# A quarter of a token tile moves from dense expert products to row gathers in a one-core transformer block

## The chip, the core and the metric

The kernel runs on one core of a Trainium2 chip. The metric is device time in microseconds. The core has TensorE (PE, matmuls; PEld is its weight load), VectorE (DVE), ScalarE (ACT), GpSimd (POOL) and SyncE (SP), and 16 DMA engines that the queues of SP and POOL feed here. Engines run their own instructions in the order in which they were placed, and wait for each other by semaphores.

## The reference

One decoder block on 1024 tokens of width 1024, all in float32: adaLN and RMSNorm, a combined projection, a pooling mixer and forgetting attention, an output projection, and then the part that matters here, a product-key expert layer:

```
def peer_ffn(h, w_query, sub_keys, expert_u, expert_v):
    # 8 heads, two halves of 128 keys; top 16 of each half, then the top 16 of their sums
    # idx: (tokens, 8, 16) out of 16384 experts; gates: softmax over each head's 16
    u = expert_u[ec]                                     # (tokens, 8, 16, 1024)
    a = gelu(einsum('cd,chkd->chk', xc, u)) * wc
    return einsum('chk,chkd->cd', a, expert_v[ec])
x = x + gt2 * peer_ffn(h2, ...);  return rmsnorm(x, final_g)
```

Each token thus uses 128 of 16384 experts; each expert is one row of `peer_u` and one of `peer_v`, 4 KB each.

## The kernel before

Tokens are held in eight tiles of 128. The program has three passes over the tokens (`PHASES`: tokens 0 to 511, 512 to 767, 768 to 1023) and then one long stage, `dense_experts`.

A pass (`phase`) does projections (`proj`, 24 matmuls for each chunk of 128 output columns; float32 products are made of three products of high and low parts, `mm3`), attention, the output projection, and the scores for the expert layer (`w_query` chunks, `keys`, top 16 of each half). The next pass's head is woven into its end. What follows from the scores comes in two ways:

- For tiles inside `DT0` to `DT1` (1 to 5, 640 tokens) the experts are computed densely. `choose(tt)` picks the 128 experts of each token, `gates(gb, tt)` builds in 32 steps a token-by-expert matrix of gates from one-hot products (PE line 978, POOL line 966, ACT line 979) and writes it to `Gd` in DRAM, 1 MB after every four steps. In the dense stage `up(e)` multiplies the 640 tokens with 128 experts' u rows (48 matmuls, two halves of `NH` = 320 columns), applies gelu, multiplies with the gates `Gg`, and splits into `ah`, `al`; `down(gr, c)` multiplies these with v rows and adds into `accT`. There are 128 of each, in 16 groups of eight `up` and eight `down`. `finish_dense` transposes the result back, normalizes and stores.
- For the other tiles (0, 6, 7) `experts(tt)` gathers: 128 indirect DMAs of one u row for each of the 128 tokens (512 KB each, line 895), each followed by a product and sum on DVE (line 910) into `dots`, then 128 of v rows with a scaled sum on DVE (line 920), and the closing norm and store. Its `h2` and `acc` lie in PSUM. Gathered rows rotate through `GBUFS` + `GMORE` = 5 row buffers.

`choose`, `gates` and `experts` are generators in a list of background work, `bg["todo"]`. Each of their yields names a cost. `tick(us)`, called after each projection, attention piece and dense unit, adds `us` times `bg["rate"]` to a credit, and background pieces are taken from the front of the list while credit is left. `drain()` takes all that remains. `RATES` are the rates: second pass, third pass, dense stage, end of the third pass. The order of the list before: in the second pass choose and gates of tiles 1 to 3 (and choose of tile 0), in the third those of tiles 4 and 5, in the dense stage choose of 6 and 7, then experts of 0, 6, 7. The framework then places instructions on each engine by a timeline of its own, and DMAs marked `keep_in_program_order` keep their order.

Weights of the dense stage are loaded by SP (`load_w`, line 244: 512 KB into one of two `wr`), copied by ACT to `wh` (line 232) and split by POOL to `wl` (line 233). POOL also issues the gathers.

Of the kernel before, what the change touches and what calls it, by code (L numbers as in the profile page):

```python
# [26 lines left out]
DT0, DT1 = 1, 6  # L27
ND = (DT1 - DT0) * 128
# [3 lines left out]
GMORE = 2  # L32
# [8 lines left out]
RATES = (0.75, 0.6, 0.68, 0.7)  # L41
# [5 lines left out]
def block_kernel(ctx: ExitStack, tc: tile.TileContext, I, out, dbg=None):  # L47
# [344 lines left out]
    def head2(c):  # L392
        n, t0 = c.n, c.t0
        c.hTh = c.big.tile([128, 8, n], R, name="hTh", tag="A")
        c.hTl = c.big.tile([128, 8, n], R, name="hTl", tag="B")
        cols = (C_F,) + ((C_U, C_GA, C_GB, C_Q) if c.p == 0 else ())
        zs = to_T(c, c.xs, None, sc1, sh1, c.hTh, c.hTl, [("w_in", i) for i in cols])
        z = zs[0]
        c.pre = dict(zip(cols[1:], zs[1:]))

        zf, e1 = (c.tile("full", 3)[:16] for _ in range(2))
        nc.scalar.activation(zf, z[:16], AF.Identity, bias=bfc)
        nc.scalar.activation(e1, zf, AF.Abs)
        nc.scalar.activation(e1, e1, AF.Exp, scale=-1.0)
        nc.scalar.activation(e1, e1, AF.Ln, bias=1.0)
        nc.vector.scalar_tensor_tensor(e1, zf, 0.0, e1, op0=OP.min, op1=OP.subtract)
        nc.vector.tensor_tensor_scan(zf, e1, e1, flast, op0=OP.add, op1=OP.bypass)
        nc.vector.tensor_copy(flast, zf[:, n - 1:n])
        nc.vector.tensor_scalar(e1, zf, -1.0, None, op0=OP.mult)
        fhl = c.big.tile([48, n], R, name="fhl", tag="fhl", bufs=1)  # L410
        fh, fl = fhl[0:16], fhl[32:48]
        split(fh, fl, e1, nc.vector)
        mv(Fd[:, 0, t0:t0 + n], fh)
        mv(Fd[:, 1, t0:t0 + n], fl)
        if dbg and "F" in dbg:
            nc.sync.dma_start(dbg["F"][:, t0:t0 + n], zf)
# [64 lines left out]
    def phase(c, nxt):  # L481
# [259 lines left out]
        dl = [i for i in range(NQ) if DT0 <= qb0 + i < DT1]  # L741
        gl = [i for i in range(NQ) if i not in dl]
        if dl:
            T = slice(dl[0] * 128, dl[-1] * 128 + 128)
            o = (qb0 + dl[0] - DT0) * 128
            mv(h2dT[0][:, :, o:o + len(dl) * 128], h2h[:, :, T])
            mv(h2dT[1][:, :, o:o + len(dl) * 128], h2l[:, :, T])
            per = D // n
            for b, v in enumerate(tiles):
                mv(x1dT[:, b * per:(b + 1) * per, o:o + len(dl) * 128], v[:, :, T])  # L750
# [52 lines left out]
    def choose(tt, mv_, mx_):  # L803
        yield 0.0
        dense = DT0 <= tt < DT1
# [54 lines left out]
        gt = sel.tile([128, PH, 16], F, name="gate", tag="gated" if dense else f"gate{tt}", bufs=1)  # L860
# [20 lines left out]
        if dbg and "idx" in dbg:  # L881
            nc.sync.dma_start(dbg["idx"][tt * 128:(tt + 1) * 128], ix)
            nc.sync.dma_start(dbg["gate"][tt * 128:(tt + 1) * 128], gate[tt])

    X = {"i": 0, "p": None}
# [13 lines left out]

    def experts(tt):  # L900
        yield 0.0
        row = g_row("row")
        nc.sync.dma_start(row, h2d[tt])
        h2 = X["ps"].tile([128, D], F, name="h2", tag="gx", bufs=1)
        nc.scalar.activation(h2, row, AF.Copy)
        dots = gp.tile([128, 128], F, name="dots", tag="dots", bufs=1)
        for k in range(128):
            yield GSTEP
            g = gather(I["peer_u"], idx[tt][:, k:k + 1])
            nc.vector.scalar_tensor_tensor(g, g, 1.0, h2, op0=OP.mult, op1=OP.mult, accum_out=dots[:, k:k + 1])  # L910
# [14 lines left out]
        r1, r2 = g_row("r1"), g_row("r2")  # L925
        nc.sync.dma_start(r1, x1d[tt])
        nc.sync.dma_start(r2, I["final_g"].partition_broadcast(128))
        nc.vector.tensor_tensor(r0, r0, r1, op=OP.add)  # L928
        ss = cst.tile([128, 4], F, name="ss", tag="ssg", bufs=2)
        nc.scalar.activation(r1, r0, AF.Square, accum_out=ss[:, 3:4])  # L930
        nc.scalar.activation(ss[:, 3:4], ss[:, 3:4], AF.Sqrt, scale=1.0 / D, bias=epsc)  # L931
        nc.vector.reciprocal(ss[:, 3:4], ss[:, 3:4])  # L932
        nc.vector.scalar_tensor_tensor(r0, r0, ss[:, 3:4], r2, op0=OP.mult, op1=OP.mult)  # L933
        nc.sync.dma_start(out[tt * 128:(tt + 1) * 128, :], r0)

    def gates(gb, tt):
# [35 lines left out]
        def use(q, o1, o2):  # L972
# [8 lines left out]
            if r == 3:  # L981
                nc.sync.dma_start(Gd[:, :, (tt - DT0) * 8 + c, :].rearrange("g p x -> p g x"),
# [3 lines left out]
        for q in range(32):  # L986
# [8 lines left out]
    def dense_experts():  # L995
# [47 lines left out]
        def finish_dense(i, rows, fg):  # L1043
            ps = [f() for f in ((pt_tile, pt_tile), (z_tile, z_tile), (s_tile, s_tile))[i % 3]]
            ss = cst.tile([128, 4], F, name="ss", tag="ssd", bufs=2)
            yt = rows[:, i * D:i * D + D]
            hs = (slice(0, 512), slice(512, 1024))
            for hf, (pt, H) in enumerate(zip(ps, hs)):
                for c in range(4):
                    nc.tensor.transpose(pt[:, c * 128:(c + 1) * 128],  # L1050
                                        acc[:, hf * 4 + c, i * 128:(i + 1) * 128], ident)
                nc.scalar.activation(yt[:, H], pt, AF.Square, accum_out=ss[:, hf:hf + 1])
            rs = rstd(ss)
# [16 lines left out]
        for i in range(DT1 - DT0):  # L1070
            finish_dense(i, rows, fg[:, 0])
# [33 lines left out]
    late = [experts(tt) for tt in range(DT0)]  # L1105
    bg["todo"] = ch[:DT0] + [f for i in range(DT0, 4) for f in (ch[i], gates(gb, i))]
# [11 lines left out]
    bg["todo"] = ch + late + [experts(tt) for tt in range(DT1, 8)]  # L1118
# [60 lines left out]
```

## Time and profile before

| | us |
|---|---|
| median of 3 runs | 3370.76 (3367.56 to 3373.42) |
| the profiled execution | 3370.09 |
| its span, first to last instruction | 3368.4 |
| mean granted TensorE clock | 0.975 of full speed |

The span is cut below into stretches. The third pass ends near 1502 us, where the first matmul of 320 columns starts; the dense matmuls end near 3320 us. Busy time of PE is modelled, since matmuls are pipelined; the rate of a stretch is read from the number of matmuls in it, or from their starts. "Idle before, releaser" is the time in which an engine waited and what ended it.

### The profile page before, as it was taken

What the parts mean: (1) busy time and instruction counts of PE and PEld (TensorE: products, weight loads), DVE (VectorE), ACT (ScalarE), POOL (GpSimd) and SP (SyncE); (2) the same over time, 40 slices, a digit from 0 to 9 for tenths busy, and PEclk for the clock granted to TensorE, in tenths of its full rate; (3) what the DMA queues carried; (4) which work ended last, traced back from release to release, by engine and by line L of the source; (5) the groups of instructions that cost most, each with busy time, mean ns of one, the idle gap of its engine ahead of it and who ended that gap; (6) DMA issues with size and microseconds to landing.
All of it is one profiled execution on the core that took longest, in us unless ns stands there. A gap on an engine that the chain in (4) does not pass through costs nothing. (4 is left out here: it accounts for less than half of the span.)

```text
span 3368.4 us, 57444 instructions
## 1 busy us (share of the span) xinstructions
PE 3153.8 (94%) x21232; PEld 3014.7 (89%) x21232; DVE 2423.6 (72%) x5472; ACT 1240.8 (37%) x2317; POOL 1756.9 (52%) x1328
## 2 busy tenths in 40 slices
PE   6999989888889899888999999999999999999995
PEld 4788778788788889888999999999999999999994
DVE  5764456988858876669766777677676766777677
ACT  5545543345554565633222322232222222322231
POOL 1233233014323132323877777688776867777774
PEclk9999999899999999999999999999999999999997
DMA  8987777767788778893899899899998999999997
GB/s 328 324 294 259 274 274 288 252 223 228 241 307 279 248 243 268 264 339 132 317 333 327 326 326 336 316 355 329 336 328 318 325 336 338 345 320 336 327 337 253
DMA packets 378840, 1004.64 MB, mean 298 GB/s; under 512 B 34768, under 2 KB 151104, under 8 KB 376384
## 3 DMA queue, kind: packets, MB, share of 16 engines
q1 hardware_dynamic: 267968, 598.26, 51.6%
q0 software_dynamic: 110592, 402.70, 33.0%
q8 instruction: 168, 2.75, 0.3%
q14 instruction: 112, 0.92, 0.1%
HBM read 851.25 MB, written 149.58 MB: 297 GB/s over the span
## 5 line engine op out<-in xcount | busy, mean ns | idle before, releaser
L233 POOL TENSOR_TENSOR wl<-wr,wh 128x1024 fp32r<-128x1024 f32 x320 | 776.5, 2427 | 624.8 <-ACT wh L232 553.1
L232 ACT ACTIVATE wh<-wr 128x1024 fp32r<-128x1024 f32 x325 | 344.2, 1059 | 900.4 <-PE oT L280 520.7
L279 PE MATMUL oT<-ah,wh 128*128 128x320 f32 x2048 | 631.9, 309 | 7.5 <-ACT ah L232 7.5
L279 PE MATMUL z<-h2x,wh 128*128 128x320 f32 x2048 | 633.1, 309 | 2.4 <-ACT wh L232 1.3
L280 PE MATMUL oT<-al,wh 128*128 128x320 f32 x2048 | 632.8, 310 | 1.6 <-DVE al L233 1.6
L280 PE MATMUL z<-h2x,wh 128*128 128x320 f32 x2048 | 632.8, 309 | 0.0
L281 PE MATMUL z<-h2x,wl 128*128 128x320 f32 x2048 | 632.6, 309 | 0.1
L281 PE MATMUL oT<-ah,wl 128*128 128x320 f32 x2048 | 632.1, 309 | 0.1
L920 DVE SCALAR_TENSOR_TENSOR acc<-g,dots,acc 128x1024 f32<-128x1024 f32 x381 | 489.7, 1285 | 139.2 <-DMA g<-peer_v,idx 136.2
L910 DVE SCALAR_TENSOR_TENSOR g<-g,h 128x1024 f32<-128x1024 f32 x384 | 461.6, 1216 | 104.0 <-DMA g<-peer_u,idx 102.7
L895 POOL DMA_INDIRECT g<-peer_u,idx x384 | 361.9, 942 | 131.2 <-issue 57.4
L895 POOL DMA_INDIRECT g<-peer_v,idx x384 | 362.0, 943 | 127.5 <-issue 49.7
L279 PEld LDWEIGHTS oT<-ah,wh 128*128 128x128 f32 x2048 | 384.4, 188 | 8.3 <-ACT ah L232 8.3
L280 PEld LDWEIGHTS oT<-al,wh 128*128 128x128 f32 x2048 | 384.6, 188 | 3.0 <-DVE al L233 3.0
L279 PEld LDWEIGHTS z<-h2x,wh 128*128 128x128 f32 x2048 | 384.4, 188 | 3.1 <-ACT wh L232 1.7
L281 PEld LDWEIGHTS oT<-ah,wl 128*128 128x128 f32 x2048 | 384.6, 188 | 0.4 <-POOL wl L233 0.4
L281 PEld LDWEIGHTS z<-h2x,wl 128*128 128x128 f32 x2048 | 384.3, 188 | 0.4 <-POOL wl L233 0.4
L280 PEld LDWEIGHTS z<-h2x,wh 128*128 128x128 f32 x2048 | 384.4, 188 | 0.0
L966 POOL TENSOR_TENSOR o<-hi,lo 128x512 f32<-128x512 f32 x160 | 206.4, 1293 | 316.2 <-PE G L978 280.9
L279 PE MATMUL z<-hTh,wh 128*128 128x256 f32 (+1 forms) x840 | 288.9, 348 | 24.5 <-ACT hTh L232 8.3
L281 PE MATMUL z<-hTh,wl 128*128 128x256 f32 (+1 forms) x840 | 287.1, 342 | 3.8 <-DMA wl<-w_inl 3.8
L280 PE MATMUL z<-hTl,wh 128*128 128x256 f32 (+1 forms) x840 | 286.7, 341 | 1.4 <-DVE hTl L233 1.3
(286 smaller groups left out, 6042.3 us busy)
## 6 DMA issues: line engine op xcount, KB each, us to landing
wr<-ut SPq DMA_DIRECT2D x128, 512.0 KB
wr<-vt SPq DMA_DIRECT2D x128, 512.0 KB
Gd<-Gb SPq DMA_DIRECT2D x40, 1024.0 KB
Gg<-Gd SPq DMA_DIRECT2D x16, 2560.0 KB
wh<-w_inh SPq DMA_DIRECT2D x60, 512.0 KB
wl<-w_inl SPq DMA_DIRECT2D x60, 512.0 KB
wm<-w_mod SPq DMA_DIRECT2D x48, 512.0 KB
wr<-w_in SPq DMA_DIRECT2D x45, 512.0 KB
```

Of the source, the lines that this page charges most:

```text
L232: nc.scalar.activation(hi, src, AF.Copy)
L233: eng_lo.tensor_tensor(lo, src, hi.bitcast(F), op=OP.subtract)
L279: nc.tensor.matmul(ps, ah, bh, start=start, stop=False)
L280: nc.tensor.matmul(ps, ah, bl, start=False, stop=False)
L281: nc.tensor.matmul(ps, al, bh, start=False, stop=stop)
L895: d = nc.gpsimd.indirect_dma_start(out=g, out_offset=None, in_=table, in_offset=bass.IndirectOffsetOnAxis(ap=col, axis=0))
L910: nc.vector.scalar_tensor_tensor(g, g, 1.0, h2, op0=OP.mult, op1=OP.mult, accum_out=dots[:, k:k + 1])
L920: nc.vector.scalar_tensor_tensor(acc, g, dots[:, k:k + 1], acc, op0=OP.mult, op1=OP.add)
L966: nc.gpsimd.tensor_tensor(o2, hi[:, X, :, None].to_broadcast([128, 4, 8, 16]), lo[:, X, None, :].to_broadcast([128, 4, 8, 16]), op=OP.mult)
```

## The change

The dense products now take tokens 32 to 639 (608 tokens, halves of 304 columns). Gathered are tiles 5, 6 and 7 and tokens 0 to 31 of tile 0 (`HT`). For that quarter tile, 32 tokens lie four times on the 128 partitions, each quarter with 32 of the token's 128 experts, so that 32 + 32 gathers do it; three SBUF moves and sums then add the quarters. Its `experts` generator stands at the end of the third pass's list (after choose and gates of tile 4), with `h2` and `acc` in SBUF (`ha`) as long as the PSUM pool is not there. `choose(5)` moves from the third pass into the dense stage, where `drain()` leaves what is left of the quarter tile too. Tile 5 is now written as rows (`x1d`, `h2d`) in the second pass's end. Tile 0's `gates` begin at step 8 of 32. `GMORE` goes from 2 to 4. Two rates change.

```
-DT0, DT1 = 1, 6
-ND = (DT1 - DT0) * 128
+DA, DB = 32, 640
+HT, DT1 = 0, 5
+HK = 32
+ND = DB - DA
-GMORE = 2
+GMORE = 4
-RATES = (0.75, 0.6, 0.68, 0.7)
+RATES = (0.75, 0.65, 0.77, 0.7)
...
-        fhl = c.big.tile([48, n], R, name="fhl", tag="fhl", bufs=1)
+        fhl = c.tile("plh", 1, R)
...
         if p == 2:
-            bg["todo"].insert(0, gates(W["gb"], DT1 - 1))
             bg["rate"] = RATES[3]
...
-        dl = [i for i in range(NQ) if DT0 <= qb0 + i < DT1]
-        gl = [i for i in range(NQ) if i not in dl]
+        lo, hi = max(t0, DA), min(t0 + n, DB)
+        gl = [i for i in range(NQ) if not DA <= t0 + i * 128 <= DB - 128]
...
-        dense = DT0 <= tt < DT1
+        dense = tt < DT1
+        gathered = tt == HT or not dense
...
+    def x_tile(name):
+        if X["ps"]:
+            return X["ps"].tile([128, D], F, name=name, tag="gx", bufs=1)
+        return gp.tile([128, D], F, name=name, tag="ha", bufs=1)
+
     def experts(tt):
         yield 0.0
+        n, K = (HK, HK) if tt == HT else (128, 128)
         row = g_row("row")
-        nc.sync.dma_start(row, h2d[tt])
-        h2 = X["ps"].tile([128, D], F, name="h2", tag="gx", bufs=1)
+        ix, gt = idx[tt], gate[tt]
+        if tt == HT:
+            ix = sel.tile([128, HK], I32, name="ixh", tag="ixh", bufs=1)
+            gt = sel.tile([128, HK], F, name="gth", tag="gth", bufs=1)
+            for b in range(128 // HK):
+                to, c = slice(b * HK, b * HK + HK), slice(b * HK, b * HK + HK)
+                nc.sync.dma_start(ix[to], idx[tt][:HK, c])
+                nc.sync.dma_start(gt[to], gate[tt][:HK, c])
+                nc.sync.dma_start(row[to], h2d[tt][:HK])
+        else:
+            nc.sync.dma_start(row, h2d[tt])
+        h2 = x_tile("h2")
...
-        for k in range(128):
+        for k in range(K):
...
+        r1 = g_row("r1")
+        if tt == HT:
+            for b in range(1, 128 // HK):
+                nc.sync.dma_start(r1[:n], r0[b * n:b * n + n])
+                nc.vector.tensor_tensor(r0[:n], r0[:n], r1[:n], op=OP.add)
+                r1 = g_row("r1")
...
-        for q in range(32):
+        for q in range(DA // 4 if tt == HT else 0, 32):
...
-    late = [experts(tt) for tt in range(DT0)]
-    bg["todo"] = ch[:DT0] + [f for i in range(DT0, 4) for f in (ch[i], gates(gb, i))]
+    early = [experts(HT)]
+    bg["todo"] = [f for i in range(4) for f in (ch[i], gates(gb, i))]
     bg["rate"] = RATES[0]
     c, ch = phase(c, next_head(2))
     W["xq"].release()
-    bg["todo"] += [f for i in range(4, DT1) for f in (ch[i - 4], gates(gb, i))][:-1]
+    bg["todo"] += [ch[0], gates(gb, 4)] + early
+    late = ch[1:]
     bg["rate"] = RATES[1]
     c, ch = phase(c, lambda: None)
+    early = [f for f in bg["todo"] if f in early]
+    bg["todo"] = [f for f in bg["todo"] if f not in early]
     drain()
...
-    bg["todo"] = ch + late + [experts(tt) for tt in range(DT1, 8)]
+    bg["todo"] = early + late + ch + [experts(tt) for tt in range(DT1, 8)]
     bg["rate"] = RATES[2]
     dense_experts()
```

The rest of the diff follows from these: `rstd` and `finish_dense` take a last tile of 96 tokens, addresses in `Gd`, `h2dT` and `x1dT` start at token 32, and the gates and indices of gathered tiles share three buffers.

## Rows read from the trace of the kernel before

**Rows 1.** The page's first section, over the whole span: busy us (share of the span) x instructions of each engine.
```profile
span 3368.4 us, 57444 instructions
PE 3153.8 (94%) x21232; PEld 3014.7 (89%) x21232; DVE 2423.6 (72%) x5472; ACT 1240.8 (37%) x2317; POOL 1756.9 (52%) x1328
```

**Rows 2.** Stretches of the span. Columns: stretch, its length, busy us (x instructions) of PE, PEld, DVE, ACT and POOL, then the granted clock, the DMA share and GB/s.
```profile
1260.00:1400.00 140.00, 134.78 (x1108) 128.91 (x1107) 94.75 (x182) 80.35 (x161) 43.61 (x37) 1.00 0.82 263
1400.00:1502.00 102.00, 85.28 (x655) 82.23 (x654) 61.80 (x249) 43.07 (x83) 24.36 (x18) 0.93 0.93 330
1502.00:1600.00 98.00, 88.00 (x575) 85.40 (x575) 97.31 (x347) 33.43 (x55) 38.11 (x20) 0.97 0.41 151
1600.00:3300.00 1700.00, 1699.44 (x11586) 1698.93 (x11585) 1221.62 (x1868) 454.37 (x737) 1282.38 (x983) 1.00 0.91 330
...
3321.00:3369.00 48.00, 6.36 (x35) 5.08 (x33) 30.43 (x42) 10.21 (x29) 11.35 (x12) 0.56 0.74 247
```

**Rows 3.** What TensorE waited for between 1502 and 3321 us, the longest entry: us in total, times, longest us.
```profile
PE oT L279 <- ACT ah L232: 7.5, 3, 5.8
```

**Rows 4.** Starts of matmuls in time order, the first and the last of four unbroken series on TensorE: 95 starts of 320 columns, 18 of 256, 17 of 256 at another place, 16 of 512. Columns: start us, duration us, engine, line, tiles, shapes.
```profile
2000.05 0.31 PE L279 MATMUL z<-h2x,wh 128*128 128x320 f32 x1
...
2013.84 0.31 PE L280 MATMUL z<-h2x,wh 128*128 128x320 f32 x1
...
1188.27 0.28 PE L279 MATMUL z<-hTh,wh 128*128 128x256 f32 x1
...
1190.28 0.28 PE L281 MATMUL z<-hTh,wl 128*128 128x256 f32 x1
...
1181.03 0.28 PE L280 MATMUL z<-hTl,wh 128*128 128x256 f32 x1
...
1182.84 0.28 PE L281 MATMUL z<-hTh,wl 128*128 128x256 f32 x1
...
332.42 0.39 PE L279 MATMUL z<-hTh,wh 128*128 128x512 f32 x1
...
335.85 0.39 PE L279 MATMUL z<-hTh,wh 128*128 128x512 f32 x1
```

**Rows 5.** Groups of instructions by line and shape between 1602 and 3300 us: count | busy us, mean ns of one | idle before, releaser.
```profile
L233 POOL TENSOR_TENSOR wl<-wr,wh 128x1024 fp32r<-128x1024 f32 x242 | 585.2, 2418 | 195.2 <-ACT wh L232 193.3
L920 DVE SCALAR_TENSOR_TENSOR acc<-g,dots,acc 128x1024 f32<-128x1024 f32 x356 | 457.6, 1285 | 127.0 <-DMA g<-peer_v,idx 124.1
L910 DVE SCALAR_TENSOR_TENSOR g<-g,h 128x1024 f32<-128x1024 f32 x380 | 456.9, 1216 | 104.0 <-DMA g<-peer_u,idx 102.7
...
L895 POOL DMA_INDIRECT g<-peer_u,idx x377 | 354.9, 941 | 125.7 <-issue 56.3 <-DVE g L910 31.0 <-DVE al L233 6.6
...
L1021 DVE TENSOR_TENSOR z<-z,Gg 128x320 f32<-128x320 f32 x240 | 118.9, 496 | 54.7 <-ACT z L1019 52.8
L233 DVE TENSOR_TENSOR al<-z,ah 128x320 fp32r<-128x320 f32 x240 | 116.7, 487 | 22.7 <-ACT ah L232 22.7
L1037 DVE TENSOR_TENSOR accT<-accT,oT 128x320 f32<-128x320 f32 x234 | 113.2, 485 | 162.3 <-PE oT L281 162.2
...
L910 DVE DVE_READ_ACCUMULATOR g<-g,h 128x1 f32 x380 | 31.5, 83 | 0.0
```

**Rows 6.** Waits between 1600 and 3300 us: VectorE for gathered v rows, GpSimd for a row buffer that VectorE still reads.
```profile
DVE acc L920 <- DMA g<-peer_v,idx: 124.1, 109, 4.3
...
POOL g L895 <- DVE g L910: 31.6, 58, 2.7
```

**Rows 7.** Two stretches of the dense stage behind the change from one gathered tile to the next; columns as in rows 2.
```profile
2200.00:2280.00 80.00, 80.00 (x547) 80.00 (x546) 62.66 (x119) 24.09 (x43) 65.59 (x51) 1.00 0.99 369
2200.00:2300.00 100.00, 100.00 (x684) 100.00 (x683) 75.87 (x143) 27.27 (x46) 80.23 (x63) 1.00 0.96 357
```

**Rows 8.** VectorE's two costliest groups from 1502 to 1600 us, both of `choose`; columns as in rows 5.
```profile
L853 DVE SCALAR_TENSOR_TENSOR cand<-pk 128x128 f32<-128x128 f32 x64 | 28.4, 598 | 0.0
L857 DVE TENSOR_REDUCE pk<-cand 128x128 f32<-128x1024 f32 x8 | 9.7, 1214 | 0.1
```

**Rows 9.** The end of the span in time order; columns as in rows 4, and in brackets the idle time before and its releaser.
```profile
3320.09 0.31 PE L281 MATMUL oT<-ah,wl 128*128 128x320 f32 x1
...
3322.81 1.29 DVE L920 SCALAR_TENSOR_TENSOR acc<-g,dots,acc 128x1024 f32<-128x1024 f32 x1 [1.18 <-DMA g<-peer_v,idx]
...
3346.93 1.40 DVE L1055 SCALAR_TENSOR_TENSOR Gg<-z,ss,h2x 128x512 f32<-128x512 f32 x2
...
3357.19 1.29 DVE L920 SCALAR_TENSOR_TENSOR acc<-g,dots,acc 128x1024 f32<-128x1024 f32 x1 [0.71 <-DMA g<-peer_v,idx]
...
3364.34 0.34 SPq L934 DMA_DIRECT2D out<-r  x1
```

**Rows 10.** The matmuls of `gates` between 1040 and 1502 us; columns as in rows 5.
```profile
L978 PE MATMUL G<-o,o 128*128 128x128 f32 x702 | 98.8, 284 | 15.4 <-ACT Gb L979 6.6 <-issue 5.5 <-POOL o L966 3.3
```

**Rows 11.** DMA issues over the whole span: count, KB each, and for the gathers the median us from issue to landing.
```profile
wr<-ut SPq DMA_DIRECT2D x128, 512.0 KB
...
Gd<-Gb SPq DMA_DIRECT2D x40, 1024.0 KB
Gg<-Gd SPq DMA_DIRECT2D x16, 2560.0 KB
...
g<-peer_u,idx POOLq DMA_INDIRECT x384, 6.2
```

More of the change, by code (lines that the diff above doesn't have):

```diff
@@ L219, in rms, with rstd @@
         return rstd(ss)
-    def rstd(ss):
+    def rstd(ss, n=128):
+        ss = ss[:n]
         nc.vector.tensor_add(ss[:, 2:3], ss[:, 0:1], ss[:, 1:2])
-        nc.scalar.activation(ss[:, 3:4], ss[:, 2:3], AF.Sqrt, scale=1.0 / D, bias=epsc)
+        nc.scalar.activation(ss[:, 3:4], ss[:, 2:3], AF.Sqrt, scale=1.0 / D, bias=epsc[:n])
         nc.vector.reciprocal(ss[:, 3:4], ss[:, 3:4])
@@ L740, in phase @@
         z0, = to_T(c, x1, rsb, sc2, sh2, h2h, h2l, [("w_query", 0)])
[L741 to L747 removed]
+        lo, hi = max(t0, DA), min(t0 + n, DB)
+        gl = [i for i in range(NQ) if not DA <= t0 + i * 128 <= DB - 128]
+        if lo < hi:
+            T = slice(lo - t0, hi - t0)
+            O = slice(lo - DA, hi - DA)
+            mv(h2dT[0][:, :, O], h2h[:, :, T])
+            mv(h2dT[1][:, :, O], h2l[:, :, T])
             per = D // n
             for b, v in enumerate(tiles):
[L750 removed]
+                mv(x1dT[:, b * per:(b + 1) * per, O], v[:, :, T])
         if gl:
@@ L859, in choose @@
             nc.vector.tensor_add(dst, dst, pf)
-        gt = sel.tile([128, PH, 16], F, name="gate", tag="gated" if dense else f"gate{tt}", bufs=1)
+        gt = sel.tile([128, PH, 16], F, name="gate", tag="gate" if gathered else "gated", bufs=3 if gathered else 1)
         nc.vector.tensor_tensor(gt, ts, ts[:, :, 0:1].to_broadcast([128, PH, 16]), op=OP.subtract)
@@ L867, in choose @@
         gf = gt.rearrange("p h k -> p (h k)")
-        if not dense or (dbg and "idx" in dbg):
-            ix = sel.tile([128, 128], I32, name=f"idx{tt}")
+        if gathered:
+            ix = sel.tile([128, 128], I32, name=f"idx{tt}", tag="idx", bufs=3)
             nc.vector.scalar_tensor_tensor(ix, w0, 128.0, w1, op0=OP.mult, op1=OP.add)
@@ L874, in choose @@
         if dense:
-            tr = W["gb"].tile([128, 3, 128], F, name="pairT", tag="pairT", bufs=DT1 - DT0)
+            tr = W["gb"].tile([128, 3, 128], F, name="pairT", tag="pairT", bufs=DT1)
             pt = pt_tile()
@@ L880, in choose @@
             pairT[tt] = tr
[L881 to L885, printed above, removed]
+    X = {"i": 0, "p": None, "ps": None}
     def g_row(name):
@@ L1041, in down, with finish_dense @@
             tick(24 * ND * 0.00043)
-        def finish_dense(i, rows, fg):
+        def finish_dense(i, yt, fg):
             ps = [f() for f in ((pt_tile, pt_tile), (z_tile, z_tile), (s_tile, s_tile))[i % 3]]
             ss = cst.tile([128, 4], F, name="ss", tag="ssd", bufs=2)
-            yt = rows[:, i * D:i * D + D]
+            T = slice(i * 128, min(i * 128 + 128, ND))
+            n = T.stop - T.start
             hs = (slice(0, 512), slice(512, 1024))
@@ L1049, in finish_dense @@
                 for c in range(4):
[L1050 to L1053, printed above, removed]
+                    nc.tensor.transpose(pt[:n, c * 128:(c + 1) * 128], acc[:, hf * 4 + c, T], ident)
+                nc.scalar.activation(yt[:n, H], pt[:n], AF.Square, accum_out=ss[:n, hf:hf + 1])
+            rs = rstd(ss, n)
             for pt, H in zip(ps, hs):
-                nc.vector.scalar_tensor_tensor(yt[:, H], pt, rs, fg[:, H], op0=OP.mult, op1=OP.mult)
-            nc.sync.dma_start(out[(DT0 + i) * 128:(DT0 + i + 1) * 128, :], yt)
+                nc.vector.scalar_tensor_tensor(yt[:n, H], pt[:n], rs, fg[:n, H], op0=OP.mult, op1=OP.mult)
+            nc.sync.dma_start(out[DA + T.start:DA + T.stop, :], yt[:n])
         for gr in range(16):
@@ L1069, in dense_experts @@
                 down(gr, i)
-        for i in range(DT1 - DT0):
-            finish_dense(i, rows, fg[:, 0])
+        for i in range((ND + 127) // 128):
+            finish_dense(i, rows[:, i * D:i * D + D] if i < 4 else fg[:, 1], fg[:, 0])
         W["m"], X["p"] = 0, None
```

31 lines of the change are left out of this document (16 added, 15 removed).

## The prediction

> **What bounds the kernel now.** I read the page's shares first. TensorE is busy 94% of a span of 3368.4 us [rows 1]; that is a mean over three passes and one long stage, so it says nothing yet about 5% fewer dense columns. The table by stage [rows 2] does. The reader should see that from 1600 to 3300 TensorE is busy 1699.4 of 1700 us, at the full granted clock, with 11,586 matmuls, 146.7 ns each, while VectorE has 28% and GpSimd 25% to spare. The waits of TensorE between 1502 and 3321 are next: the longest entry is 7.5 us in 1819 [rows 3]. So the dense stage is matmul rate and nothing else. Its 12,288 matmuls of 320 columns (128 units `up`, 128 units `down`, 48 each) make 1802 us.
>
> Two other stretches are not so bound. From 1502 to 1600 VectorE is busy 97.3 of 98 us, DMA only 0.41 [rows 2]. After 3321 TensorE is done, and 48 us follow in which gathers of the last expert tile run on [rows 2, 9]. In the end of the third pass (1400 to 1502) the DMA share is 0.93 at 330 GB/s, with TensorE idle 17 us [rows 2].
>
> **The change, part by part.** All sums are against the profiled execution: 3370.1 us, 1.7 over its span, 0.7 under the median of the runs.
>
> *Dense columns, 640 to 608.* Each half goes from 320 to 304 columns; the count of matmuls stays. 94 steps between starts of 320-column matmuls take 13.79 us, 146.7 ns; 17 steps at 256 columns take 2.01 us, 118.2 ns; in another spot 16 steps take 1.81 us, 113.1 ns; 15 steps at 512 columns take 3.43 us, 228.7 ns [rows 4]. The slopes are 0.445 (from 118.2), 0.525 (from 113.1) and 0.427 ns a column (up to 512), so 16 columns are worth 7.1, 8.4 or 6.8 ns. I take 7.1, since both its ends lie next to 304: 12,288 x 7.1 = **87 us less**, bounds 84 and 103. The Trainium skill (TensorE: Matmul & The Clock Gate, "Wait — 56ns, not 53.3ns?") puts a warm matmul at its columns over 2.4 GHz plus about 2.5 ns. That would be 135.8 ns at 320, which the trace contradicts with 146.7; by the rule's slope alone the term would be 82 us.
>
> *The tail.* `tick` gives background work credit; 0.68 x 24 x 640 x 0.00043 x 256 = 1150 before. Two `choose` (24.0 each by their yields) and three expert tiles (257 x 1.46 = 375.2 each) cost 1174: 24 short, 16 gathers left over. The trace agrees: the last dense matmul starts at 3320.1, and accumulations from gathers run from 3322.8 to 3358.5, the closing rows to the store at 3364.3 [rows 9]. After, the credit is 0.77 x 24 x 608 x 0.00043 x 256 = 1237 against 3 x 24 + 1125.7 + about 4 left of the quarter tile = 1202, so the list ends some 7 units (49 us) before the matmuls. What then follows the matmuls is `finish_dense`. It is interleaved with gathers until 3348.3 [rows 9]; alone I estimate 20 us for five tiles and the last store, against 48: **28 less** (20 to 31).
>
> *A third `choose` at the stage's start.* `choose(5)` moves there from the third pass. Two of them fill VectorE from 1502 to 1600: 97.3 us [rows 2], of which sixteen halves of `up` take 16 x 0.98 = 15.7 [rows 5], gathers and copies some 6, the last top-k some 11 (estimates from the first steps of the stage); 65 remain, 32 each, the two largest lines alone 38.1 for both [rows 8]. At credit 4.83 a unit a choose spreads over 5 units (33 us of TensorE). The first `down` needs all eight `up`; in those 54 us VectorE has 1.6 x 32 + 8 x 2 = 67 us; before it was 1.5 x 32 + 16 = 64 in 56. TensorE waited for this chain (7.5 us for `ah`, [rows 3]). Bounds 0 and 32 (the whole choose exposed); I take **8 more**, near the measured wait.
>
> *Gathers per unit.* Count in the stage: 768 as before. But a unit lasts 6.70 us instead of 7.04 and carries 4.83 / 1.46 = 3.31 gathers instead of 3.08. GpSimd: a split of 2.42 plus 3.31 x 0.94 = 5.5 us, 83%. VectorE: 3.31 x 1.29 + 1.4 (four such instructions in `up`, two in `down`, a little shorter at 304 columns) = 5.7 us, 85% [rows 5]. Bytes: 0.524 MB of weights, 3.31 x 0.524 of rows, 2.49 / 16 of gates with 304 columns [rows 11] = 2.415 MB, 360 GB/s; the same count for before gives 327, and the trace shows 330 [rows 2]. Has the DMA side this much? After a change of tile it ran 80 us at 369 GB/s, 100 us at 357, with TensorE busy throughout and five buffers [rows 7]. At 369 a unit needs 6.54 us, nothing lost; at 357, 6.76, 0.06 x 232 units = 14. I take **10 more**. This is the term with the widest bounds (rivals). The seven buffers cost nothing by themselves: the work that hides a late row is the buffers' own depth, 7 / 0.494 per us = 14 us against 5 / 0.437 = 11 before. With five, gathers waited on VectorE for a buffer 31.6 us in the u halves [rows 6]; without cover these waits would sit in front of the weight splits, which queue on GpSimd behind the gathers.
>
> *The quarter tile in the third pass.* By the credits: passes two and three give 187 and 133 + 42 = 176. The new list (4 choose, 120 gate steps; then choose, 32 gate steps, 64 gathers) leaves 29 at the end of pass two and begins the gathers after 85 of the 133, about 64% into the main part, near 1270 us; some 62 of 64 are through by 1502. They add 62 x 0.524 = 32.5 MB. `gates(5)` is gone from there, tile 0's 24 steps come earlier, so perhaps 6 MB of `Gd` writes (1 MB per four steps, [rows 11]) leave the stretch: 26 MB more on 36.8 + 33.7 [rows 2]. At 369 GB/s 96.5 MB are 262 us where there are 242: +20 if nothing spills; some spills into 1502 to 1580, where DMA is idle. Bounds 0 and 20 from bytes; +15. On three buffers a gather turns round in 6.2 (issue to landing, [rows 11]) + 0.9 + 1.3 = 8.4 us, 2.8 each; asked for is one in 3.5 to 4 us of real time (64 in 230 us). Removed: 8 gate steps of 8 matmuls; 702 of these cost 98.8 us [rows 10], some 1.1 us a step, so -8. VectorE gains 62 x 1.29 = 80 and loses a choose, 32, in a stretch where it is busy 65% [rows 2]; hidden. Together **7 more**.
>
> *Small ones.* Tile 5 is now also written as rows in pass two: eight transposes, about 1 us, the DMAs hidden in a pass that does not wait for SP. The quarter tile ends in three partition moves through SP, each waiting for a VectorE sum, weight loads queued behind: 3 x about 4 us, with two weight buffers (13 us) as cover. If that cover is gone it costs 12. **3 more.** Other edits (`rstd` with n, tags, `fhl` as `plh`) cost nothing: they rename space or shorten instructions that wait for nobody.
>
> Sum: -87 - 28 + 8 + 10 + 7 + 3 = -87. Span 3281, time **3283 us**.
>
> **Rivals.**
> *1. The gather stretch of the dense stage becomes DMA's.* For it: 360 GB/s asked, DMA share already 0.91 at 330 [rows 2], 0.99 at 369 [rows 7], and VectorE's 124 us of waiting for v rows [rows 6]. Against it: those same 80 us at 369 with no wait. If the sustained rate is 350, a unit takes 6.90, 0.20 x 232 = 46 instead of 10: 3319; with stalls of VectorE behind late rows up to 3345. The Trainium skill (DMA: Bandwidth & Descriptors, Specifications) gives about 358 GB/s as the HBM limit of one core. By that figure the unit would be 6.75 us and the loss 11 us, an estimate; the 80 us at 369 and the rule don't agree, though that stretch is short.
> *2. Late rows hold VectorE in the third pass.* Only three buffers there, and DMA share 0.93 at the end [rows 2]. If landings go from 6.2 to 10 us, a turn is 12.2, 4.1 each against 3.6 asked: 62 x 0.5 = 31, and each wait stands before top-k and softmax steps that TensorE waits for. Time about 3320 to 3335.
> *3. The other side: the mean traffic of before is the ceiling.* Same place, the gather stretch: at 330 GB/s a unit is 7.32 us, 0.62 x 232 = 144 in place of 10: 3417. It decides from 2.415 / (6.70 + 97 / 232) = 339 GB/s down; below it the kernel is slower. Against: 357 over 100 us [rows 7].
> *4. The narrower matmuls don't run faster* (the step is set by something besides columns, say the weight load). Then the 87 are missing: 3370, no change. Against: 256 columns step at 113 to 118 ns with the same load [rows 4].
>
> **How the numbers follow.** Forecast (TensorE stays the bound in the stage) 0.66, its own range 3250 to 3315; rival 1 0.14; rival 2 0.08; rival 3 0.05; rival 4 0.03; more gain than summed (113 ns slope, no start-up loss, under 3250) 0.04. A measurement here tells 0.2%, 7 us. Rivals 1 and 2 and the better case still end faster: about 0.90 faster, 0.03 same, 0.07 slower. The range takes in the forecast and most of rivals 1 and 2: 3250 to 3345, leaving out the rest.
>
> **What would show it.** Right: steps between 304-column matmuls near 139.6 ns and some 720 matmuls per 100 us; TensorE waits in the stage under 30 us; 350 GB/s or more while gathers run; no gather after the last dense matmul, the tail near 20 us; the stage beginning 0 to 15 us later than 1502; 60 or so gathers before it. Wrong: TensorE waiting for weight splits behind gathers (rivals 1, 3), VectorE idle for rows between 1270 and 1510 (rival 2), steps of 146 ns (rival 4), or gathers still running after the last matmul, which would mean that the list did not drain as the credits say.

## The result, and the profile after

The changed kernel takes 3412.16 us (median of 4 runs, 3407.89 to 3414.82) against 3370.46 of the kernel before: ratio 1.0124, 95% interval 1.011 to 1.0138. It is slower, where 3283 was forecast. The profiled execution took 3407.89 us; the page of after, first section [rows 1]:

```profile
span 3406.2 us, 57601 instructions
...
PE 3111.4 (91%) x21176; PEld 2961.8 (87%) x21176; DVE 2489.1 (73%) x5568; ACT 1228.9 (36%) x2324; POOL 1818.7 (53%) x1383
```

The stretches of after, columns as in [rows 2], cut at its own borders: the first 304-column matmul starts at 1537.2, the last at 3387.7.

```profile
1260.00:1400.00 140.00, 127.87 (x1009) 121.55 (x1007) 92.15 (x186) 76.98 (x164) 45.31 (x40) 0.95 0.89 291
1400.00:1537.00 137.00, 99.53 (x668) 92.24 (x666) 89.27 (x296) 32.81 (x78) 40.81 (x34) 0.85 0.98 367
1537.00:1800.00 263.00, 230.01 (x1547) 226.14 (x1548) 251.12 (x639) 70.67 (x115) 156.58 (x108) 0.94 0.72 248
1800.00:3290.00 1490.00, 1436.00 (x10123) 1430.09 (x10122) 1105.87 (x1673) 393.30 (x651) 1163.62 (x908) 0.98 0.95 346
3290.00:3388.00 98.00, 91.43 (x636) 90.81 (x635) 55.82 (x80) 23.61 (x39) 45.62 (x30) 0.95 0.58 208
3388.00:3406.00 18.00, 5.20 (x40) 3.99 (x38) 9.28 (x22) 7.36 (x25) 0.00 (x0) 0.79 0.37 139
```

The span grew by 37.8 us, in three parts. The stage begins 35.4 later (1537.2 against 1501.8). The tail is 30 shorter (18.5 against 48; the last gather is issued at 3323.4). The stage itself is 32.2 longer: 1850.5 between its first and last matmul against 1818.3. That last number hides two large ones. Undisturbed steps, from the start of one matmul to the next, went from 146.67 to 139.34 ns (means over the steps under 160 ns), which gives 90 us back over 12,288; but everything above these steps, the *loss* from here on, grew from 16.2 to 138.4.

By group (16 units, 768 matmuls; loss is the group's length less 768 undisturbed steps) the kernel before lost 15 us in group 0 and 1 in all others. The changed kernel loses 49 in groups 0 and 1, and 89 in groups 2 to 15, in every group but group 2. Groups 2 and 3 of after, cut in their `up` and `down` halves:

```profile
1800.20:1853.70 53.50, 53.50 (x386) 53.50 (x385) 43.51 (x84) 19.74 (x38) 45.98 (x37) 1.00 0.97 350
1853.70:1907.30 53.60, 53.60 (x386) 53.43 (x385) 35.29 (x67) 9.33 (x10) 42.21 (x34) 1.00 0.98 370
1907.30:1960.80 53.50, 53.50 (x386) 53.50 (x385) 42.51 (x83) 19.05 (x37) 44.21 (x35) 1.00 0.95 340
1960.80:2021.80 61.00, 56.20 (x386) 55.96 (x385) 41.32 (x45) 10.48 (x12) 44.44 (x36) 0.94 0.93 338
```

53.5 us is 384 steps of 139.3 ns, without loss. The fourth line is the pattern of nearly all later groups: the `up` half is clean, the `down` half stalls once, and the clock is lowered behind the stall. What TensorE waited for from 1800 to 3300 in after, longest entry (before: 0.6 us in the same window, and 7.5 us for `ah` at the stage's start, [rows 3]):

```profile
PE oT L285 <- POOL wl L237: 50.6, 15, 6.1
```

One such stall, the one of group 4, in the timeline of after (columns as in [rows 9]; L896 is a gather, L1033 the load of the next group's gates, L939 the sum over v rows, L1063 the add of a `down` result, L236 and L237 the two weight splits):

```profile
2076.13 0.94 POOL L896 DMA_INDIRECT g<-peer_v,idx  x1 [0.30 <-issue]
...
2076.60 0.33 SPq L1033 DMA_DIRECT2D Gg<-Gd  x1
...
2088.61 1.29 DVE L939 SCALAR_TENSOR_TENSOR acc<-g,dots,acc 128x1024 f32<-128x1024 f32 x1 [1.04 <-DMA g<-peer_v,idx]
...
2090.85 1.06 ACT L236 ACTIVATE wh<-wr 128x1024 fp32r<-128x1024 f32 x1 [9.77 <-DMA wr<-vt]
...
2092.59 0.47 DVE L1063 TENSOR_TENSOR accT<-accT,oT 128x304 f32<-128x304 f32 x1 [2.32 <-PE oT L285]
...
2095.65 0.47 DVE L1063 TENSOR_TENSOR accT<-accT,oT 128x304 f32<-128x304 f32 x1 [2.59 <-PE oT L285]
...
2095.87 0.30 PE L284 MATMUL oT<-al,wh 128*128 128x304 f32 x1
...
2096.03 6.58 DVE L939 SCALAR_TENSOR_TENSOR acc<-g,dots,acc 128x1024 f32<-128x1024 f32 x5
...
2097.59 0.93 POOL L896 DMA_INDIRECT g<-peer_v,idx  x1 [6.49 <-DVE acc L939]
...
2098.54 2.35 POOL L237 TENSOR_TENSOR wl<-wr,wh 128x1024 fp32r<-128x1024 f32 x1
...
2100.95 0.42 PE L285 MATMUL oT<-ah,wl 128*128 128x304 f32 x1 [4.79 <-POOL wl L237]
...
2101.20 0.43 PE L283 MATMUL oT<-ah,wh 128*128 128x304 f32 x1
```

Read it from the top. The 2.49 MB load goes out at 2076.60. The gather issued just before it lands 12.4 us later (the sum at 2088.61 ends its wait), where 6.2 is the median [rows 11]; the weights behind it on SP's queue land 9.8 us after ScalarE began to wait. Now VectorE, which takes its work in order, has sums of late rows to do between the adds of `down`: it first stands twice for TensorE (2.32 and 2.59), while the rows for its next sums land, and its five sums come in one piece from 2096.03. Only then is a row buffer free for the gather that GpSimd has been holding for 6.49 us, and the weight split `wl`, ready to go since 2091.9, is queued behind that gather. TensorE waits 4.79 us for it and goes on in steps of 0.25 us, at a granted clock of 0.50.

### The profile page after: what moved, and what is told of

It reads as the page before. It is cut to its first block, busy times and chain, and to the rows that moved or that the text cites. A ratio compares the mean times of both kernels' runs of the same rounds, so it can differ in the third digit from the quotient of the medians.

```text
span 3406.2 us, 57601 instructions
## 1 busy us (share of the span) xinstructions
PE 3111.4 (91%) x21176; PEld 2961.8 (87%) x21176; DVE 2489.1 (73%) x5568; ACT 1228.9 (36%) x2324; POOL 1818.7 (53%) x1383
## 4 chain that ended last, share of the span: by engine, by line
PE 45%; DVE 13%; DMA 8%; issue 6%; POOL 5%; ACT 2%; SPq 0%; POOLq 0%; DVEq 0%; ACTq 0%
PE z L283 8%; PE z L285 8%; PE z L284 8%; PE oT L285 6%; PE oT L283 5%; PE oT L284 5%; POOL g L896 3%; PE G L1004 3%; POOL wl L237 2%; DVE cand L857 2%; DMA g<-peer_v,idx 2%; DVE g L929 2%; DMA wl<-w_queryl 1%; DMA wr<-vt 1%; DVE acc L939 1%
## 5 line engine op out<-in xcount | busy, mean ns | idle before, releaser
L237 POOL TENSOR_TENSOR wl<-wr,wh 128x1024 fp32r<-128x1024 f32 x320 | 776.6, 2429 | 436.1 <-ACT wh L236 368.5
L285 PE MATMUL oT<-ah,wl 128*128 128x304 f32 x2048 | 614.1, 308 | 50.7 <-POOL wl L237 50.6
L283 PE MATMUL z<-h2x,wh 128*128 128x304 f32 x2048 | 620.5, 304 | 20.1 <-DVE al L237 14.9
L283 PE MATMUL oT<-ah,wh 128*128 128x304 f32 x2048 | 626.4, 308 | 9.6 <-ACT wh L236 7.5
L284 PE MATMUL oT<-al,wh 128*128 128x304 f32 x2048 | 626.3, 307 | 5.1 <-DVE al L237 5.1
L284 PE MATMUL z<-h2x,wh 128*128 128x304 f32 x2048 | 618.6, 303 | 0.0
L236 ACT ACTIVATE wh<-wr 128x1024 fp32r<-128x1024 f32 x325 | 342.9, 1056 | 757.4 <-DMA wr<-vt 434.7
L285 PE MATMUL z<-h2x,wl 128*128 128x304 f32 x2048 | 603.2, 303 | 10.2 <-POOL wl L237 10.0
L939 DVE SCALAR_TENSOR_TENSOR acc<-g,dots,acc 128x1024 f32<-128x1024 f32 x412 | 540.6, 1312 | 11.6 <-DMA g<-peer_v,ixh 4.7
L929 DVE SCALAR_TENSOR_TENSOR g<-g,h 128x1024 f32<-128x1024 f32 x416 | 499.3, 1216 | 37.7 <-DMA g<-peer_u,idx 21.3
L896 POOL DMA_INDIRECT g<-peer_v,idx x384 | 361.6, 942 | 167.2 <-DVE acc L939 94.2
L896 POOL DMA_INDIRECT g<-peer_u,idx x384 | 361.9, 943 | 157.1 <-issue 54.5
L283 PEld LDWEIGHTS oT<-ah,wh 128*128 128x128 f32 x2048 | 395.6, 193 | 10.9 <-ACT wh L236 8.4
L284 PEld LDWEIGHTS oT<-al,wh 128*128 128x128 f32 x2048 | 395.3, 193 | 6.0 <-DVE al L237 6.0
L283 PE MATMUL z<-hTh,wh 128*128 128x256 f32 (+1 forms) x840 | 289.2, 349 | 20.5 <-ACT hTh L236 8.2
L1063 DVE TENSOR_TENSOR accT<-accT,oT 128x304 f32<-128x304 f32 x240 | 112.4, 470 | 256.2 <-PE oT L285 253.8
```

The source lines that it names most:

```text
L236: nc.scalar.activation(hi, src, AF.Copy)
L237: eng_lo.tensor_tensor(lo, src, hi.bitcast(F), op=OP.subtract)
L283: nc.tensor.matmul(ps, ah, bh, start=start, stop=False)
L284: nc.tensor.matmul(ps, ah, bl, start=False, stop=False)
L285: nc.tensor.matmul(ps, al, bh, start=False, stop=stop)
L896: d = nc.gpsimd.indirect_dma_start(out=g, out_offset=None, in_=table, in_offset=bass.IndirectOffsetOnAxis(ap=col, axis=0))
```

## The experiments

Three theories for groups 2 to 15: the one large load (burst); the DMA's mean rate, some 346 GB/s, as ceiling (mean); GpSimd's order with its waits for row buffers (order). For the late start and groups 0 and 1: the quarter tile itself, or the gates and the third `choose` that were moved. One table for all runs, from the starts of their matmuls and gathers; "per row" is the mean distance of the 768 whole-tile gathers. The times are medians of 4 or 5 runs for before, after, the gates in pieces, before at rate 0.71 and the eighth, of one run for the others; the other columns come from one trace of each.

| run | us | stage begins | loss, groups 0-1 | loss, groups 2-15 | GB/s 1750-3250 | us per row |
|---|---|---|---|---|---|---|
| before | 3370.5 | 1501.8 | 15 | 1 | 330 | 2.31 |
| after | 3412.2 | 1537.2 | 49 | 89 | 345 | 2.17 |
| gates load in six pieces | 3396.9 | 1541.1 | 53 | 78 | 346 | 2.16 |
| gates loaded once | 3340.0 | 1543.1 | 51 | 14 | 337 | 2.08 |
| half rows | 3317.7 | 1523.6 | 46 | 18 | 233 | 2.07 |
| half products on VectorE | 3390.7 | 1527.4 | 47 | 84 | 346 | 2.15 |
| five buffers | 3412.0 | 1534.7 | 50 | 0 | 336 | 2.26 |
| rate 0.70 | 3441.4 | 1535.6 | 53 | 5 | 340 | 2.29 |
| no quarter tile | 3343.5 | 1501.8 | 12 | 99 | 340 | 2.17 |
| quarter in the stage | 3443.9 | 1506.9 | 12 | 107 | 341 | 2.17 |
| one product of three | 3274.9 | 1530.2 | - | - | 361 | 2.05 |
| before, rate 0.71 | 3341.0 | 1499.5 | 15 | 0 | 335 | 2.26 |
| an eighth tile | 3400.2 | 1509.8 | 16 | 0 | 337 | 2.18 |

**The gates load in pieces.**

```
-  if e % 8 == 0: load Gg of the group
+  if gr < 15 and c >= 2: load a sixth of the next group's Gg behind the weight load of down c
```

> The changed kernel; only the load of the next group's gates (2.4 MB, one transfer on SP's queue between the weight loads of the fifth and sixth unit down of a group) is cut in six pieces, one behind each of six weight loads. Burst theory (the one big transfer delays the weight loads queued behind it, and TensorE has less slack in a unit of 6.7 us than in one of 7.04): the stall of some 5 us with half-clock matmuls behind it, once in each down half, goes; loss per group in groups 3 to 15 falls from about 7 us to 0 to 2, time 3412 - 80 = 3325 to 3345. Mean theory (the sustained DMA rate of 345 GB/s is the ceiling): the bytes are the same, the loss is only spread over all units, time 3400 to 3415. GpSimd-order theory (weight splits wait behind gathers that wait for a row buffer): no change, 3405 to 3415.

Ratio to before 1.0066 (1.005 to 1.0083): some 15 us better than the change, not 80. The waits of TensorE from 1800 to 3290 show what became of the stalls:

```profile
PE oT L285 <- POOL wl L237: 24.0, 25, 2.4
PE z L285 <- POOL wl L237: 19.2, 20, 2.0
```

They are smaller, more, and now in the `up` halves too, as the mean theory had it. Burst in the narrow sense (the place in SP's queue) falls.

**The gates loaded once**, to ask about the same bytes another way.

```
-  if e % 8 == 0: load Gg
+  if e == 0: load Gg
```

> The changed kernel with the gates of the dense products loaded once, for the first group, and used for all sixteen: the dense experts are then weighted with wrong gates from group 1 on, and 15 loads of 2.4 MB are gone. By the counts a group asks for 8 x (0.524 + 3.33 x 0.524) = 18.2 MB in each half of 53.5 us, 339 GB/s, and 2.49 MB more in its down half, 386; with the loads gone both halves ask for 339. Theory that the down half asks for more than the queues carry (370 GB/s where TensorE asked for nothing): groups 2 to 15 lose under 15 us in all, where they lost 89; groups 0 and 1 keep their 49; time 3412 - 75 = 3330 to 3350. Rival, that the rows and the weights alone are too much at this rate (row waits on GpSimd, seven rows in flight): they still lose 50 us or more, 3370 to 3400.

As expected: 14 us of 89 are left, though 93% of the traffic and every gather, split and sum stay. TensorE is busy 1480.9 of 1490 us from 1800 to 3290, and its longest entry of waiting there is:

```profile
PE oT L285 <- POOL wl L237: 3.8, 2, 2.0
```

**Half rows, and half products.**

```
-  gather table[ix] -> g (4 KB a row)              +  gather half a row, 2 KB, used twice (u products into a tile of their own)
-  product, sum over g[:, :1024] (other kernel)    +  over g[:, :512]
```

> The changed kernel, but each gather fetches 2 KB of a row in place of 4 KB (the first index range of the same tables, half a row each); the products on VectorE take the half twice, at their full size. So the rows that are multiplied are not those of the reference, and row traffic is halved everywhere, in the third pass too; the count of gathers, of VectorE's instructions and the 2.4 MB loads stay. Both DMA theories (burst and mean): the dense stage loses its stalls, loss over 12,288 x 139.3 ns falls from 138 to under 40 us; time about 3290 to 3320, less if the passes gain too (if the passes' 35 us are row traffic: 3260 to 3285). GpSimd-order theory: loss stays over 100 us, time over 3390.

> The changed kernel with the products of VectorE over gathered rows cut to 512 of their 1024 columns, so the expert layer of the gathered tokens takes in half of each row; every transfer stays. What it is to tell: whether VectorE's load makes the loss at the start of the dense stage (groups 0 and 1 lose 49 us in the changed kernel, as much with halved rows, 12 without the quarter tile). VectorE theory: groups 0 and 1 lose 12 to 28, stage begins 5 to 15 us earlier, time 3412 - 35 = 3365 to 3390. DMA or order theory: 45 or more stay. In both the later groups keep 60 to 95 us, since the bytes are the same; if these go too, late row buffers behind VectorE made them, 3310 to 3340.

With half the bytes of the rows and the same GpSimd and VectorE work the loss in groups 2 to 15 falls to 18; with half of VectorE's work on rows and the same bytes it stays at 84. So order and VectorE's load are how a late transfer reaches TensorE, not why it is late. Groups 0 and 1 answer to neither, 46 and 47 (so the whole loss with half rows is 64, where under 40 was expected): neither the bytes of the rows nor their products alone make the loss at the start. The stage begins 14 and 10 us earlier in the two.

**Five buffers, and a lower rate.**

```
-  GMORE = 4                       +  GMORE = 2
-  RATES[2] = 0.77                 +  RATES[2] = 0.70   (other kernel)
```

> The changed kernel with five row buffers in the dense stage, as before, in place of seven. Theory that seven outstanding row transfers crowd out the weight loads: the loss in the down halves shrinks, 3350 to 3385. Burst and mean theories: at most seven rows in flight were never the point; VectorE waits more for rows, GpSimd more for buffers, time equal or longer, 3405 to 3440. GpSimd-order theory: fewer buffers, more waits in front of the weight splits, 3420 to 3480.

> The changed kernel, seven row buffers, with the background rate of the dense stage at 0.70 in place of 0.77: 3.01 gathers in a unit, 2.26 MB in 6.70 us, 337 GB/s. If the rate that is asked for makes the loss (not the seven buffers): groups 2 to 15 lose under 15 us, but some 53 gathers are left for after the last matmul, a tail of 100 to 140 us, time 3385 to 3420, much like the run with five buffers. If the seven buffers make it: the groups still lose 50 us or more, 3430 to 3470.

Five buffers don't make the order ask for less by the credits, but gathers are placed later with them (the planner seems to place one where it sees a buffer free): 68 come after the last weight split, 55 with the lower rate (none in after). In both the stage is clean from group 2 on, so neither seven buffers nor GpSimd's queue hurt by themselves; it is the rate asked for. The gain is spent at once on the tail. Five buffers, stage and tail:

```profile
1800.00:3290.00 1490.00, 1489.99 (x10707) 1489.64 (x10706) 1084.23 (x1675) 420.10 (x684) 1150.39 (x873) 1.00 0.93 335
3290.00:3395.00 105.00, 11.83 (x77) 10.67 (x76) 90.98 (x90) 9.00 (x26) 59.05 (x63) 0.57 0.94 339
```

The price for the run at 0.70 was too low (3441, not 3385 to 3420): its tail moved only 243 GB/s.

**What the DMA can do.**

```
-  mm3: three products            +  in the dense stage only the product of the high parts
```

> The changed kernel, but in the dense stage each of its matmul triples keeps only the product of the two high parts; the two correction products are left out, so the dense experts are computed at lower precision. Every load, split, gather and VectorE step stays. A unit is then some 2.3 us of TensorE, so TensorE asks for nothing and the stage runs as fast as its transfers, GpSimd (5.5 us a unit) or VectorE (5.7 us a unit) allow. Mean theory (about 346 GB/s is the DMA's own ceiling in this mixture): 340 to 355 GB/s while gathers and weight loads run together, share 0.94 or more, a unit with its gathers still 6.8 to 7.1 us. Rival (the traffic of the changed kernel stopped at 346 because of how the work is ordered around TensorE's units, the queue having more to give): 365 GB/s or more, a unit under 6.65 us.

Both theories were half right. In 100-us stretches between the changes of tile it carries 367 to 375 GB/s, at a share of 0.97 to 0.99; that, not 346, is the limit for this mixture of rows, weights and gates. Over 1500 us it is 361, since each change of tile costs some traffic:

```profile
1750.00:3250.00 1500.00, 802.60 (x3495) 746.64 (x3496) 1209.03 (x1865) 413.17 (x679) 1207.21 (x952) 0.70 0.96 361
...
2100.00:2200.00 100.00, 56.19 (x236) 51.97 (x235) 78.53 (x92) 25.77 (x42) 80.91 (x64) 0.68 0.99 374
2200.00:2300.00 100.00, 50.85 (x240) 47.95 (x240) 72.28 (x135) 29.88 (x49) 76.69 (x60) 0.74 0.95 350
```

**The quarter tile, left out and moved.**

```
-  early = [experts(HT)]           +  early = []
-  in the third pass's list        +  behind the three choose in the stage's list   (other kernel)
```

> The changed kernel without the gathered experts of the quarter tile: the expert layer of tokens 0 to 31 is not computed. Everything else stays, also the longer list of gates in the second pass. If the quarter tile's 64 gathers and their sums are what lengthens the third pass (+21 us) and the start of the dense stage (groups 0 and 1 lose 49 us, 15 before), both go: stage begins near 1515, groups 0 and 1 lose 15 to 25, time 3412 - 45 = 3355 to 3375. If the shifted gates (24 steps of tile 0 moved into the second pass) and three choose at the start of the stage do it: stage begins at 1535, groups 0 and 1 lose 40 to 50, time 3400 to 3412. The second pass should keep its +22 us in either case.

> The changed kernel with the quarter tile's experts moved out of the third pass: they follow the three choose in the dense stage's list, before the three whole tiles (four index and gate buffers in place of three). Without them the stage should begin at 1502 and its groups 0 and 1 lose 10 to 15 us, as in the run without the quarter tile: 35 + 37 us come back. What the 64 gathers then cost in the stage: mean theory: 33.5 MB more at 346 GB/s, on a stretch that is at the ceiling already, 97 us less the DMA's slack after the last gather (some 60 us at 0.6 of the ceiling, worth 25 us), so 3406 - 72 + 75 = 3395 to 3420 with 20 to 40 gathers left for after the last matmul. If the place in the third pass was the fault, and the stage only had bad order: 3345 to 3370.

Without it the stage begins at 1501.8, as before the change, and groups 0 and 1 lose 12, with three `choose` at the start. So the quarter tile costs all of the 35 us of the passes and 37 in groups 0 and 1; the third `choose` and the moved gates cost nothing in sum (within the passes the same matmuls come up to 14 us earlier or 28 later than before). The whole gain, 69 us, is more than the 45 expected. In the stage its 64 gathers cost 100 us, most of it as a longer tail (3443.9 against 3343.5), more than the price of 75: 33.5 MB at the 341 GB/s of that run are 98. The place in the third pass was the better of the two.

**Two other splits of the work.**

```
-  RATES[2] = 0.68 (before)        +  RATES[2] = 0.71
-  DA, DB = 32, 640; HK = 32       +  DA = 16, HK = 16, halves of 320 and 304, GMORE = 3, rate 0.76   (from after)
```

> The kernel before with one number changed: the background rate of the dense stage is 0.71 in place of 0.68, so that the credit is 1200 against a list of 1174, and no gather should be left after the last dense matmul. Asked for is 0.524 + 3.22 x 0.524 + 0.164 = 2.37 MB in a unit of 7.04 us, 337 GB/s, under the 346 that the changed kernel reached. Mean theory: no loss in the stage, the tail goes from 48 to about 20 us: 3370 - 28 = 3340 to 3348. If the stage already stalls at 337: losses of some us in each down half, 3355 to 3375.

> Half of the change, placed by what the other runs say: an eighth of a token tile (16 tokens, eight experts of a token on 128 partitions, 16 + 16 gathers) leaves the dense products (624 columns, halves of 320 and 304), its experts follow the three choose in the dense stage, six row buffers, background rate 0.76. Asked for is about 346 GB/s over the gather stretch. Mean theory: TensorE's part falls by 12,288 x 7.1 / 2 = 44 us, DMA is just at its ceiling, so stalls of 10 to 40 us or a tail that is that much longer: 3370 - 44 - 28 + 25 = 3310 to 3345. If the stage stalls at this rate as in the changed kernel: 3345 to 3375.

The first is faster than both kernels: 3341.03 us, ratio 0.9912 (0.9897 to 0.9928). Groups 2 to 15 take 112.6 us each, with no loss, and no gather is left for the tail:

```profile
1600.00:3300.00 1700.00, 1699.79 (x11589) 1699.53 (x11589) 1245.63 (x1883) 458.66 (x736) 1300.54 (x1001) 1.00 0.93 335
3317.00:3336.00 19.00, 6.76 (x42) 5.83 (x40) 10.41 (x24) 8.85 (x28) 0.00 (x0) 0.73 0.42 166
```

The eighth is slower than before, 1.0086 (1.0072 to 1.0101): 3400.16 us, over both forecasts. Its stage has no loss after group 1, but 75 gathers come after its last weight split, 100 us at 382 GB/s:

```profile
1750.00:3250.00 1500.00, 1500.00 (x10516) 1500.00 (x10515) 1090.56 (x1710) 416.32 (x681) 1152.66 (x883) 1.00 0.93 337
3280.00:3380.00 100.00, 6.08 (x30) 4.36 (x28) 96.19 (x93) 8.32 (x25) 64.08 (x70) 0.53 0.99 382
```

## Why the prediction was wrong

**Right: the matmul term and the tail.** 12,288 x (146.67 - 139.34) = 90 for 87. The Trainium skill's slope (TensorE: Matmul & The Clock Gate, "Wait — 56ns, not 53.3ns?") gave 82; the trace, at 0.458 ns a column, sides with the slope between 256 and 320 columns, 0.445 [rows 4]. The tail shrank by 30 for 28, and no gather was left, as the credits said.

**The step that failed: the room on the DMA, the 10 us of *Gathers per unit*.** The prediction spread the gates load over 16 units (2.49 / 16), got 360 GB/s for every unit, and took 369 seen for 80 us [rows 7] as room enough. That stretch was a reading of the limit, not of room to spare: there the DMA was at 0.99 [rows 7]. Over 1500 us, with the changes of tile, the same mixture carried 361 even where TensorE did a third of its matmuls. The demand (the bytes moved in a half, over the half's undisturbed length) in groups 2 to 14 of after was 366 GB/s on the mean, and not even: the gates load lies in the `down` half alone, so a `down` half asked for 393 (median), an `up` half for 339. So the 10 us of that term were 88.

The other runs bear it out. Those that lost under 9 us in groups 2 to 14 (before, before at rate 0.71, an eighth, five buffers, rate 0.70, gates loaded once) asked for 331 to 342 on the mean and 339 to 357 in a `down` half; those that lost 70 to 100 (after, gates in pieces, half products, no quarter tile, quarter in the stage) for 364 to 366 and 377 to 395. So it is shown that the DMA was asked for too much. Whether the mean or the peak in the `down` half decides is not shown. For the peak: after lost 76 us in the 13 `down` halves of these groups and 4 in their `up` halves. Against it: with the load in six pieces the halves asked for 357 and 377 and lost 35 us each. By bytes alone the loss would be 19 us by the mean (366 against 361), 43 by the `down` halves (393 against 370); both are estimates. The rest would be the loop in the timeline (VectorE, GpSimd and TensorE waiting for each other in order) and the half clock behind each stall. And not all of the loss is bytes: half rows, at 236 GB/s, still lost 18.

Ten of the 89 us have another cause. Group 15 has no gates to load, and its `down` half loses 9.7 at a DMA share of 0.38. The list of gathers now ends before the matmuls, so the closing steps of the last gathered tile fall into this half. ScalarE stands 20.5 us for one of them, until 3348.08, with the next weight copy `wh` placed behind it, and TensorE waits 5.4 and 1.2 us for `wh`. With the gates loaded once, 5.5 of the 14 us that are left lie there.

**The rivals.** Rival 1 named the place (weight splits late, DMA-bound) and with 3319 to 3345 undersized it: 46 us in the gather stretch, where 88 came. Rival 3 came out near the measured time, 3417, but by another way: the traffic did not stay at 330, it rose to 346, above the 339 at which that rival was to stop mattering. At 346 its own formula gives a unit of 6.98 us, 0.28 x 232 = 65 and 3338; the rest came from the passes, the start and the larger loss. That 3417 lies near 3412 is luck.

**The quarter tile: 7 forecast, 35 measured, and 34 more in groups 0 and 1.** The list was to reach it at 1270, with 62 gathers done by 1502. Its first gather runs at 1360.0, and 45 are issued before the stage's first split; the rest (to 1621) and the closing moves fall into groups 0 and 1. The stretch from 1400 to 1537 is at 0.98 and 367 GB/s: the DMA full a second time, with TensorE's clock at 0.85. The bounds (0 to 20 from bytes) left out that late gathers hold VectorE's order, rival 2's mechanism: from 1260 to 1537 VectorE stood nine times for its u rows, 15.8 us. Half rows take back 14 of the 35, half products 10; how the rest comes about is open. The three closing moves, reckoned at 3 x about 4 us, each waiting for a sum, went out within 1.3 us instead; moves and sums took 10 us together.

**The third `choose`: 8 forecast, nothing measured**: with three of them and without the quarter tile groups 0 and 1 lose 12, before 15.

**Left open.** Groups 0 and 1 lose 49 with the quarter tile and 12 without, whatever the size of its rows or products (46, 47). TensorE waits there, longest of all for `al`, behind sums, top-k steps and the closing moves on a VectorE that is 95% busy; which of these orders costs how much wasn't told apart. A load of the gates in the `up` half wasn't tried, since their one buffer is in use there. Leaving the quarter's work out altogether gives 3343.5, no better than the kernel before at rate 0.71: in these runs narrower products are worth nothing while 768 rows go with them at this limit. Rows went at 2.05 us each where TensorE did a third of its matmuls; whether an order that keeps the demand flat would find time here is not shown, and the six pieces, a step that way, won 15 us.

## What to carry to other kernels

Reckon the demand of the whole loop and of each half or phase in which a large load lies, and hold the first against what the mixture carries over a long stretch, the second against the best that a short one shows; a stretch at a share of 0.99 shows the limit of its mixture, not room. A demand equal to that limit leaves nothing for the waits of one engine on another. When an engine-bound stage is speeded up by 5%, everything that rides along (weights, rows) must go 5% faster too, so the room on the next resource is the whole gain that can be had. And clear the plain loss first: the 29 us of the tail took one changed number, the rate, without moving any work.

## What the runs showed of the hardware

Sums on VectorE with all operands in SBUF collide with GpSimd's splits. In the quarter tile the accumulator lies in SBUF: 21 of its 31 sums, those that overlap no split, took 1.27 us; the 10 that overlap one took 2.52, up to 3.71. With the accumulator in PSUM the 186 sums that overlap a split took 1.28, at most 1.29. From the timeline of after:

```profile
1552.68 2.41 POOL L237 TENSOR_TENSOR wl<-wr,wh 128x1024 fp32r<-128x1024 f32 x1 [0.90 <-ACT wh L236]
...
1553.35 2.82 DVE L939 SCALAR_TENSOR_TENSOR acc<-g,dots,acc 128x1024 f32<-128x1024 f32 x1 [1.54 <-DMA g<-peer_v,ixh]
...
1556.75 1.26 DVE L939 SCALAR_TENSOR_TENSOR acc<-g,dots,acc 128x1024 f32<-128x1024 f32 x1
...
1558.98 3.71 DVE L939 SCALAR_TENSOR_TENSOR acc<-g,dots,acc 128x1024 f32<-128x1024 f32 x1
...
1559.24 2.36 POOL L237 TENSOR_TENSOR wl<-wr,wh 128x1024 fp32r<-128x1024 f32 x1
```

The sum of 1553.35 lasts until 1.08 us after the split's end, that of 1558.98 until 1.09 after. The Trainium skill (SBUF — State Buffer, Who interferes with whom) says that a VectorE instruction with two SBUF inputs contends with a GpSimd instruction that reads SBUF; the trace agrees, with 1.27 against 2.52 us. The 10 sums cost 12 us of VectorE's time that no term held. One core moved 367 to 375 GB/s through many stretches of 100 us, and more for shorter ones, where the prediction quoted a limit of about 358 from the Trainium skill (DMA: Bandwidth & Descriptors, Specifications). The highest of after, columns as in [rows 2]:

```profile
2880.00:2917.00 37.00, 36.13 (x256) 35.64 (x256) 25.08 (x46) 6.36 (x7) 29.64 (x23) 1.00 1.01 406
```

So even a share of 0.99 gives different rates in different mixtures, and the limit in the argument above is one read off the dense stage's own.
